# Pairs of heads, feature-major rotary queries and a shorter row of 1/rms in a two-layer attention trunk

## The chip, the cores and the metric

One core of one Trainium2 chip runs the whole program. The metric is the time of one execution on the device in microseconds, as the median of several runs. The kernel before takes 1045.22 us (median of 3 runs, 1045.22 to 1045.81).

## The reference

The input is 256 tokens of width 2048, in float32. Two layers follow each other; each has a mixer, a gate, a residual and a small per-layer embedding.

```
h = rms_norm(x); y = (mixer(h) * silu(gate(h))) @ w_out
x = x + rms_norm(y); x = x + (p @ w_pp) * sigmoid(x @ w_pg)
```

Mixer A (16 heads of 128) is stick-breaking attention without a softmax: with z the scaled scores, a key s before a query t has the weight exp(z - softplus(z) - the sum of softplus(z) over the keys between them). Mixer B (16 heads) is latent attention: queries and keys are made from normalised latents of rank 512, and each score is the sum of a 128-wide product and a 64-wide rotary product, whose key is shared by all heads:

```
q_rope = [t1 * cos - t2 * sin, t1 * sin + t2 * cos]
s = (q_nope . k_nope + q_rope . k_rope) * scale; softmax over the keys of the query's chunk and before
```

## The kernel before, in words

All matrix products that matter run in split precision: a float32 operand becomes a high part (float32r, rounded by ScalarE) and a low part (VectorE subtracts), and a product is high x high, high x low and low x high. The weights come from HBM in units of 128 x 1024 (`unit()`, lines 89 to 106): SP issues the load into one of four `raw` buffers, ScalarE makes `whi` (line 82), VectorE `wlo` (line 83); of each there are four.

Two forms of product use them. `rows()` (line 113) keeps tokens on the partitions: three matmuls (`mm3`, lines 109 to 111) with activations as the stationary operand. `cols()` (line 123) has features on the partitions: the weights are stationary and the activations move, high and low parts side by side, so that a pair of matmuls of 512 columns (line 133) and 256 columns (line 135) does the same. `halves()` (lines 146 to 151) then adds the two halves of the bank: a copy by ScalarE and a sum by VectorE.

TensorE's results go into eight banks of PSUM: four `acc` for the large products and four `att` for attention and transposes.

Layer 0: gate groups, then four groups of four heads (`group_a`, lines 355 to 368), each with 24 units of weights. Layer 1: the latents, gate groups, then four groups of four heads (`group_b`, lines 571 to 602): two units of `w_uk`, two of `w_uq`, one of `w_uqr` (the rotary queries) and two of `w_uv`. The heads of a group are worked while the next group's large products run: `weave()` (line 156) takes the products as a stream that yields after each unit, and the heads as jobs of three stages, and calls job i's stage s when `at[i] + s * LAG` units are through. The last group's heads run under the first units of the output product (`residual`, line 405).

A head of mixer A (`stick_breaking`, lines 329 to 353): scores in plain float32 (lines 333 and 334; a plain float32 matmul runs as two passes), two masks in bf16 (lines 335 and 336); ScalarE and VectorE make softplus(z), split as `sph` and `spl`; the triangle of -1 (`trir`) times both adds the sums over later keys of a block, and `nones` (all -1, plain float32) times `sp` those of the next block (line 349); exp gives the weights, `weighted_v` (line 321) the output, and `finish_head` (line 316) multiplies by the gate and splits.

A head of mixer B (`mla`, lines 539 to 569): scores in plain float32 (lines 543 and 544), masks (545 and 546), the rope product as four matmuls in float32r (548 and 549), softmax by row, transposes of the probabilities (line 565), weighted values.

The rotary queries of a group (lines 578 to 599): `rows()` leaves them with tokens on the partitions, `rotate()` (line 487) turns them in four VectorE instructions for each half of the tokens, the result is split into `qhl`, and eight transposes (line 597) bring it into feature-major form, from where ScalarE casts it into `qr`:

```
for j in range(2):
    for t in range(NT):
        nc.tensor.transpose(b[:, j * T + t * P:j * T + (t + 1) * P],
                            qhl[t][:, 2 * i + j].rearrange("p i r -> p (i r)").bitcast(F32), ident)
nc.scalar.copy(qr[:, 2 * i:2 * i + 2, :], pair(b))
```

`rstd_row()` (lines 217 to 227) lays 1/rms of the tokens along the free axis, on all partitions: ones times a diagonal, twice, so that the row stands there for two heads. It is called twice.

What orders the work: the kernel is written for a framework that keeps dependencies, buffers and semaphores. Its planner gives each engine a fixed order of instructions (`schedule_with_timeline_sim=True`, line 699): the written order is the priority, but an instruction whose operands the planner expects late by its own timing is put behind others of that engine that it expects ready. On the chip each engine then works through its order and waits where an operand is not there. The DMAs are almost all issued by SP, in such an order too.

## Time and profile before

| | us |
|---|---|
| median of the runs | 1045.22 |
| the profiled execution, its time | 1045.87 |
| its span in the profile | 1044.1 |
| busy: TensorE, VectorE, ScalarE | 1035.8, 630.6, 567.4 |

The span is the time from the first to the last instruction on the core; the execution's time has 1.8 us more around it. In the rows, PE is TensorE (its matmuls), PEld its weight loads, DVE VectorE, ACT ScalarE, POOL GpSimd and SP SyncE, which issues the transfers; a q behind the name is the engine's sequencer. L597 is line 597 of the kernel. Matmuls overlap, so a matmul's duration is longer than the distance to the next one.

### The profile page before, as it was taken

How to read it: one execution, taken by the hardware profiler on the slowest of the kernel's cores; microseconds unless marked ns; L12 is line 12 of the kernel's file. 1: busy time of each engine (PE TensorE's matmuls, PEld its weight loads, DVE VectorE, ACT ScalarE, POOL GpSimd, SP SyncE). 2: the span in 40 equal slices, each digit the busy share in tenths (PEclk: the TensorE clock that was granted, in tenths of full speed). 3: DMA queues.
4: the chain of work that ended last, by engine and by line, in shares of the span. 5: the costliest groups of instructions: out<-in, count | busy, mean ns of one | idle time of the engine just before them, and what ended most of it. 6: DMA issues, size and time to landing. Idle time of an engine off the chain costs nothing.

```text
span 1044.1 us, 14568 instructions
## 1 busy us (share of the span) xinstructions
PE 1035.8 (99%) x5563; PEld 890.4 (85%) x5563; DVE 630.6 (60%) x912; ACT 567.4 (54%) x888; POOL 6.9 (1%) x10
## 2 busy tenths in 40 slices
PE   8999999999999999999999999999999999999998
PEld 6888888888888888888888898888888888888888
DVE  7465564555655655556665576666777765558553
ACT  7654444554555556545655555665666654446442
POOL 0000000000000000000000000000000000000000
PEclk9999999999999999999999999999999999999999
DMA  8856465555555554564655485555544344655662
GB/s 305 307 169 198 166 218 185 165 173 166 163 174 168 171 191 142 180 205 150 222 181 185 129 243 185 178 191 182 183 141 136 108 150 151 205 188 183 217 209 77
DMA packets 55813, 189.03 MB, mean 181 GB/s; under 512 B 6208, under 2 KB 6976, under 8 KB 55744
## 3 DMA queue, kind: packets, MB, share of 16 engines
q1 hardware_dynamic: 55600, 188.09, 55.5%
q8 instruction: 43, 0.70, 0.3%
q14 instruction: 26, 0.21, 0.1%
q10 hardware_dynamic: 144, 0.02, 0.0%
HBM read 185.99 MB, written 2.10 MB: 180 GB/s over the span
## 4 chain that ended last, share of the span: by engine, by line
PE 96%; DMA 2%; DVE 1%; ACT 0%; issue 0%; SPq 0%; DVEq 0%
PE acc L133 24%; PE acc L109 17%; PE acc L111 17%; PE acc L110 17%; PE acc L135 12%; PE att L325 1%; DMA raw<-in_w_in_a_dram 1%; PE att L191 1%; DMA x<-in_x_dram 1%; PE att L544 1%; PE att L333 1%; PE att L326 1%; PE att L549 1%; PE att L565 0%; PE att L109 0%; PE att L111 0%
## 5 line engine op out<-in xcount | busy, mean ns | idle before, releaser
L83 DVE TENSOR_TENSOR wlo<-raw,whi 128x1024 fp32r<-128x1024 f32 (+1 forms) x295 | 355.9, 1217 | 279.9 <-ACT whi L82 272.1
L82 ACT ACTIVATE whi<-raw 128x1024 fp32r<-128x1024 f32 (+1 forms) x295 | 308.1, 1053 | 272.8 <-PE acc L111 173.3
L133 PE MATMUL acc<-actT,whi 128*128 128x512 f32 x1024 | 356.1, 398 | 1.7 <-ACT whi L82 1.1
L111 PE MATMUL acc<-whi,actT 128*128 128x512 f32 (+2 forms) x736 | 277.6, 379 | 0.0
L109 PE MATMUL acc<-whi,actT 128*128 128x512 f32 (+2 forms) x736 | 277.1, 378 | 0.0
L110 PE MATMUL acc<-wlo,actT 128*128 128x512 f32 (+2 forms) x736 | 277.0, 377 | 0.0
L135 PE MATMUL acc<-actT,wlo 128*128 128x256 f32 x1024 | 273.2, 281 | 0.1
L133 PEld LDWEIGHTS acc<-actT,whi 128*128 128x128 f32 x1024 | 189.2, 188 | 40.9 <-ACT whi L82 2.6
L135 PEld LDWEIGHTS acc<-actT,wlo 128*128 128x128 f32 x1024 | 192.6, 189 | 6.1 <-DVE wlo L83 0.7
L110 PEld LDWEIGHTS acc<-wlo,actT 128*128 128x128 f32 x736 | 138.5, 188 | 24.3
L109 PEld LDWEIGHTS acc<-whi,actT 128*128 128x128 f32 x736 | 138.4, 188 | 24.0
L111 PEld LDWEIGHTS acc<-whi,actT 128*128 128x128 f32 x736 | 138.2, 188 | 23.9
L87 DVE SCALAR_TENSOR_TENSOR wlo<-raw,pre,whi 128x512 fp32r<-128x512 f32 x80 | 55.6, 749 | 31.4 <-ACT whi L86 31.4
L86 ACT ACTIVATE whi<-raw,pre 128x512 fp32r<-128x512 f32 x80 | 52.0, 713 | 32.5 <-PE acc L133 20.0
L150 ACT COPY half<-acc 128x256 f32<-128x256 f32 x96 | 34.6, 367 | 35.3 <-PE acc L135 33.4
L133 PE MATMUL acc<-latT,whi 128*128 128x512 f32 x128 | 46.2, 401 | 0.0
L135 PE MATMUL acc<-latT,wlo 128*128 128x256 f32 x128 | 36.0, 282 | 0.0
L133 PEld LDWEIGHTS acc<-latT,whi 128*128 128x128 f32 x128 | 24.0, 188 | 5.7 <-DVE arena L151 0.4
L135 PEld LDWEIGHTS acc<-latT,wlo 128*128 128x128 f32 x128 | 24.2, 189 | 0.1
L82 ACT ACTIVATE actT<-y 128x256 fp32r<-128x256 f32 x32 | 13.3, 418 | 19.6 <-DVE y L318 19.3
L109 PE MATMUL acc<-whi,latT 128*128 128x256 f32 (+1 forms) x64 | 21.8, 340 | 0.0
L557 ACT ACTIVATE pr<-att,st 128x128 f32<-128x128 f32 (+1 forms) x32 | 13.3, 424 | 15.6 <-DVE st L555 15.6
(230 smaller groups left out, 849.2 us busy)
## 6 DMA issues: line engine op xcount, KB each, us to landing
raw<-in_w_in_a_dram SPq DMA_DIRECT2D x127, 512.0 KB, 4.2
raw<-in_w_in_b_dram SPq DMA_DIRECT2D x40, 512.0 KB, 4.4
raw<-in_w_out_a_dram SPq DMA_DIRECT2D x32, 512.0 KB, 3.6
raw<-in_w_pg_a_dram SPq DMA_DIRECT2D x32, 512.0 KB, 3.5
raw<-in_w_out_b_dram SPq DMA_DIRECT2D x32, 512.0 KB, 3.5
raw<-in_w_pg_b_dram SPq DMA_DIRECT2D x24, 512.0 KB, 4.1
raw<-in_w_dkv_dram SPq DMA_DIRECT2D x16, 288.0 KB, 3.0
raw<-in_w_pp_dram SPq DMA_DIRECT2D x8, 512.0 KB, 3.5
```

Source lines behind the costliest of these rows:

```text
L82: nc.scalar.activation(hi, src, AF.Copy)
L83: nc.vector.tensor_tensor(lo, src, hi.bitcast(F32), ALU.subtract)
L86: nc.scalar.activation(hi, src, AF.Copy, scale=gain)
L87: nc.vector.scalar_tensor_tensor(lo, src, gain, hi.bitcast(F32), ALU.mult, ALU.subtract)
L109: nc.tensor.matmul(out, lhsT=sh, rhs=mh, start=start, stop=False, **kw)
L110: nc.tensor.matmul(out, lhsT=sh, rhs=ml, start=False, stop=False, **kw)
L111: nc.tensor.matmul(out, lhsT=sl, rhs=mh, start=False, stop=stop, **kw)
L133: nc.tensor.matmul(o, lhsT=hi[:, c], rhs=aT[2][:, k].rearrange("p i t -> p (i t)"), start=k == 0, stop=False, skip_group_check=True)
L135: nc.tensor.matmul(o[:, :T], lhsT=lo[:, c], rhs=aT[0][:, k, :], start=False, stop=k == ktot - 1, skip_group_check=True)
L150: nc.scalar.copy(b, o[:, T:])
L191: nc.tensor.transpose(b[:, kk * T + t * P:kk * T + (t + 1) * P], x[:, t, k * P:(k + 1) * P], ident)
L557: nc.scalar.activation(pr[:, c], s[:, c], AF.Exp, scale=SCALE_B, bias=st[:, 1, t:t + 1], accum_out=st[:, 2, t:t + 1])
```

## The change

1. Heads go in pairs. A job is two heads, the jobs are two for each group, and `weave()` starts job i's stage s at `(i + s) * lag + 1`, with a lag of 6 units in layer 0 and of 2 in layer 1. In a stage the two heads' matmuls of one kind stand together: scores of both, masks of both, and so on. `weighted_v` puts both heads in one bank and `finish_pair` treats them in one step.
2. `nones` becomes float32r and is multiplied with `sph` and `spl` in place of `sp`.
3. The rotary queries are made feature-major: the product with `w_uqr` runs in the form of `cols()`, with the weights' columns sorted (in the split, by `by_half`) so that the first halves of the four heads' queries fill one bank and the second halves the other; the rotation is two products with a feature-major table `ropeT`, a subtraction and an addition; sixteen DMAs of 32 partitions (32 KB each) from SBUF to SBUF bring each head's halves to their partitions in `qs`, twice; `qr` is the rounded copy, its lower half of the partitions replaced by the rest. `ropeT` is made once by four transposes.
4. `rstd_row` makes the row once; those who use it broadcast it.
5. Some buffers change in number: `t256` 3 to 2, `sp` 2 to 1, `sph` and `spl` 1 to 2.

```diff
...
-    def unit(src, n=UNIT, gains=None, parts=1):
+    def unit(src, n=UNIT, gains=None, parts=1, by_half=False):
...
-        if gains is None:
+        if by_half:
+            nc.sync.dma_start(out=raw, in_=src)
+            src = raw.rearrange("p (k h i r) -> p i k h r", h=GRP, i=2, r=ROPE // 2)
+            dh, dl = (z.rearrange("p (k i h r) -> p i k h r", h=GRP, i=2, r=ROPE // 2) for z in (hi, lo))
+            for i in range(2):
+                split(dh[:, i], dl[:, i], src[:, i])
+        elif gains is None:
...
         for i, o in enumerate(banks):
-            b = tmp.tile([P, T], F32, tag="t256", name="half", bufs=3)
+            b = tmp.tile([P, T], F32, tag="t256", name="half", bufs=2)
             nc.scalar.copy(b, o[:, T:])
             nc.vector.tensor_tensor(dst[:, i, :], o[:, :T], b, ALU.add)
 
...
-    def weave(stream, jobs, at):
+    def weave(stream, jobs, lag):
+
 
         n = 0
-        steps = sorted((at[i] + s * LAG, i) for i in range(len(jobs)) for s in range(STAGES))
+        steps = sorted(((i + s) * lag + 1, i) for i in range(len(jobs)) for s in range(STAGES))
         for when, i in steps:
             while n < when and next(stream, stream) is not stream:
                 n += 1
...
         for t in range(NT):
             dg = tmp.tile([P, P], F32, tag="diag", name="diag", bufs=1)
             nc.vector.tensor_scalar(dg, ident, r[:, t:t + 1], None, ALU.mult)
-            for i in range(2):
-                nc.tensor.matmul(b[:, i * T + t * P:i * T + (t + 1) * P], lhsT=ones, rhs=dg, start=True, stop=True)
-        o = tmp.tile([P, 2, T], F32, tag="rrow", name="rrow", bufs=2)
-        nc.vector.tensor_copy(o, pair(b))
+            nc.tensor.matmul(b[:, t * P:(t + 1) * P], lhsT=ones, rhs=dg, start=True, stop=True)
+        o = tmp.tile([P, 1, T], F32, tag="rrow", name="rrow", bufs=2)
+        nc.vector.tensor_copy(o[:, 0], b[:, :T])
         return o
...
     def gate_out(g, sg, row):
         for i in range(2):
             h = sg[:, GRP * g + 2 * i:GRP * g + 2 * i + 2, :]
-            nc.vector.tensor_tensor(h, h, row, ALU.mult)
+            nc.vector.tensor_tensor(h, h, row.to_broadcast([P, 2, T]), ALU.mult)
...
+    nones = const.tile([P, P], F32R, name="nones")
+    nc.vector.tensor_scalar(nones, ones, -1.0, None, ALU.mult)
...
+    def finish_pair(h, o, sg, yT):
+        hs = slice(h, h + 2)
+        y = tmp.tile([P, 2, T], F32, tag="t512", name="y", bufs=2)
+        nc.vector.tensor_tensor(y, pair(o), sg[:, hs, :], ALU.mult)
+        split(yT[0][:, hs, :], yT[1][:, hs, :], y)
+
+    def weighted_v(v, hh, ws):
+
+        o = att()
+        for i, w in enumerate(ws):
+            c = slice((hh + i) * HD, (hh + i + 1) * HD)
+            nc.tensor.matmul(o[:, i * T:(i + 1) * T], lhsT=v[:, 0, c], rhs=w[:, :T], start=i == 0, stop=False, skip_group_check=True)
+            nc.tensor.matmul(o[:, i * T + P:(i + 1) * T], lhsT=v[:, 1, c], rhs=w[:, T:], start=False, stop=i == 1, skip_group_check=True)
         return o
...
+        zs = [att()[:, :W3] for _ in range(2)]
+        for i, z in enumerate(zs):
+            mm(z[:, :T], lhsT=k[:, hh + i, :P], rhs=q[:, hh + i, :], start=True, stop=False, skip_group_check=True)
+            mm(z[:, T:], lhsT=k[:, hh + i, P:], rhs=q[:, hh + i, P:], start=False, stop=False, skip_group_check=True)
+        for z in zs:
+            mm(z[:, :P], lhsT=identb, rhs=masks[:, :P], start=False, stop=False, skip_group_check=True)
+            mm(z[:, T:], lhsT=identb, rhs=masks[:, :P], start=False, stop=True, skip_group_check=True)
...
+            sp = tmp.tile([P, W3], F32, tag="sp", name="sp", bufs=1)
+            nc.vector.scalar_tensor_tensor(sp, z, 0.0, e, ALU.max, ALU.add)
+            sph = tmp.tile([P, W3], F32R, tag="sph", name="sph", bufs=2)
+            spl = tmp.tile([P, W3], F32R, tag="spl", name="spl", bufs=2)
+            split(sph, spl, sp)
+            parts.append((sph, spl))
         yield
-        mm(z, lhsT=trir, rhs=sph, start=False, stop=False, skip_group_check=True)
-        mm(z, lhsT=trir, rhs=spl, start=False, stop=False, skip_group_check=True)
-        mm(z[:, P:T], lhsT=nones, rhs=sp[:, T:], start=False, stop=True, skip_group_check=True)
-        w = tmp.tile([P, W3], F32, tag="w", name="w", bufs=2)
-        nc.scalar.activation(w, z, AF.Exp)
+        ws = []
+        for z, both in zip(zs, parts):
+            for x_ in both:
+                mm(z, lhsT=trir, rhs=x_, start=False, stop=False, skip_group_check=True)
+            for x_ in both:
+                mm(z[:, P:T], lhsT=nones, rhs=x_[:, T:], start=False, stop=x_ is both[1], skip_group_check=True)
...
-        finish_head(h, weighted_v(v, hh, w), sgA, yT)
+        finish_pair(h, weighted_v(v, hh, ws), sgA, yT)
...
-        weave(group_a(g, q, k, v), jobs, (1, 7, 13, 19))
-        jobs = [stick_breaking(g * GRP + hh, hh, q, k, v) for hh in range(GRP)]
+        weave(group_a(g, q, k, v), jobs, 6)
+        jobs = [stick_breaking(g * GRP + hh, hh, q, k, v) for hh in range(0, GRP, 2)]
...
-        weave(out01(range(6)), jobs, (1, 2, 4, 6))
+        weave(out01(range(6)), jobs, 2)
...
+    ropeT = [tmp.tile([P, 1, T], F32, tag="sph", name="ropeT", bufs=2) for _ in range(2)]
+    b = att()
+    for t in range(NT):
+        rt = tmp.tile([P, 2, GRP, ROPE // 2], F32, tag="t256", name="rt", bufs=2)
+        half = rope[:, t, :, ROPE // 2:].rearrange("p i (o r) -> p i o r", o=1)
+        nc.vector.tensor_copy(rt, half.to_broadcast([P, 2, GRP, ROPE // 2]))
+        for i in range(2):
+            nc.tensor.transpose(b[:, i * T + t * P:i * T + (t + 1) * P], rt[:, i].rearrange("p h r -> p (h r)"), ident)
+    for i in range(2):
+        nc.vector.tensor_copy(ropeT[i][:, 0], b[:, i * T:(i + 1) * T])
...
-    arena = big.tile([P, 2, NB], F32, tag="actT", name="arena", bufs=2)
+    arena = big.tile([P, 2 * NB + GRP * T], F32, tag="actT", name="arena", bufs=2)
+    qs = arena[:, 2 * NB:].rearrange("p (h t) -> p h t", h=GRP)
     qrT = big.tile([P, 2, GRP, T], F32R, tag="tok", name="qrT", bufs=3)
...
+        ss = [att()[:, :W3] for _ in range(2)]
+        for i, s in enumerate(ss):
+            mm(s[:, :P], lhsT=q[:, hh + i, :P], rhs=k[:, hh + i, :P], start=True, stop=False, skip_group_check=True)
+            mm(s[:, P:], lhsT=q[:, hh + i, P:], rhs=k[:, hh + i, :], start=False, stop=False, skip_group_check=True)
+        for s in ss:
+            mm(s[:, P - CHUNK:P], lhsT=identb, rhs=masks[:, P:], start=False, stop=False, skip_group_check=True)
+            mm(s[:, W3 - CHUNK:], lhsT=identb, rhs=masks[:, P:], start=False, stop=False, skip_group_check=True)
+        for i, s in enumerate(ss):
+            qp = qr[:, hh + i, :]
+            for n in range(2):
+                mm(s[:, :P], lhsT=qp[:, :P], rhs=krT[:, n, :P], start=False, stop=False, skip_group_check=True)
+                mm(s[:, P:], lhsT=qp[:, P:], rhs=krT[:, n, :], start=False, stop=n == 1, skip_group_check=True)
...
-        w = unit(a["w_uqr"][g])
-        o = [acc()[:, :T], acc()[:, :T]]
-        rows(o, cqT, w, 0, NR, T, NR)
-        qrt = tmp.tile([P, NT, GRP, ROPE], F32, tag="t512", name="qrt", bufs=2)
-        qhl = []
-        for t in range(NT):
-            rotate(qrt[:, t], o[t].rearrange("p (h r) -> p h r", h=GRP), t, GRP)
-            qhl.append(tmp.tile([P, GRP, 2, ROPE], F32R, tag="rrow", name="qhl", bufs=2))
-            split(qhl[t][:, :, 0, :], qhl[t][:, :, 1, :], qrt[:, t])
+        w = unit(a["w_uqr"][g], by_half=True)
+        o = [acc(), acc()]
+        for i, b in enumerate(o):
+            for kk in range(NR):
+                whi, wlo = (z[:, kk * T + i * P:kk * T + (i + 1) * P] for z in w)
+                nc.tensor.matmul(b, lhsT=whi, rhs=cqT[2][:, kk].rearrange("p i t -> p (i t)"), start=kk == 0,
+                                 stop=False, skip_group_check=True)
+                nc.tensor.matmul(b[:, :T], lhsT=wlo, rhs=cqT[0][:, kk, :], start=False, stop=kk == NR - 1,
+                                 skip_group_check=True)
+        qrt = tmp.tile([P, 2, T], F32, tag="t512", name="qrt", bufs=2)
+        halves(qrt, o)
+        rc = tmp.tile([P, 2, T], F32, tag="rrow", name="rc", bufs=2)
+        rs = tmp.tile([P, 2, T], F32, tag="rrow", name="rsn", bufs=2)
+        for z, i in ((rc, 0), (rs, 1)):
+            nc.vector.tensor_tensor(z, qrt, ropeT[i].to_broadcast([P, 2, T]), ALU.mult)
+        nc.vector.tensor_tensor(rc[:, 0, :], rc[:, 0, :], rs[:, 1, :], ALU.subtract)
+        nc.vector.tensor_tensor(rc[:, 1, :], rc[:, 1, :], rs[:, 0, :], ALU.add)
+        for hh in range(GRP):
+            for i in range(4):
+                r = slice(i * ROPE // 2, (i + 1) * ROPE // 2)
+                nc.sync.dma_start(out=qs[r, hh, :], in_=rc[hh * ROPE // 2:(hh + 1) * ROPE // 2, i % 2, :])
+        nc.scalar.activation(qr, qs, AF.Copy)
+        nc.vector.tensor_tensor(qr[ROPE:], qs[ROPE:], qr[ROPE:].bitcast(F32), ALU.subtract)
...
-        for i in range(GRP // 2):
-            b = att()
-            for j in range(2):
-                for t in range(NT):
-                    nc.tensor.transpose(b[:, j * T + t * P:j * T + (t + 1) * P],
-                                        qhl[t][:, 2 * i + j].rearrange("p i r -> p (i r)").bitcast(F32), ident)
...
-        weave(group_b(g, q, qr, k, v), jobs, (1, 3, 5, 6))
-        jobs = [mla(g * GRP + hh, hh, q, qr, k, v) for hh in range(GRP)]
+        weave(group_b(g, q, qr, qs, k, v), jobs, 2)
+        jobs = [mla(g * GRP + hh, hh, q, qr, k, v) for hh in range(0, GRP, 2)]
...
```

## Rows read from the trace of the kernel before

**Rows 1.** The page, part 1: busy us (share of the span), instructions.

```profile
PE 1035.8 (99%) x5563; PEld 890.4 (85%) x5563; DVE 630.6 (60%) x912; ACT 567.4 (54%) x888; POOL 6.9 (1%) x10
```

**Rows 2.** The chain of waits that ended last: share of the span by engine.

```profile
PE 96%; DMA 2%; DVE 1%; ACT 0%; issue 0%; SPq 0%; DVEq 0%
```

**Rows 3.** Busy time by stretch: us (instructions) of each engine, granted clock, DMA.

```profile
750.00:800.00 50.00, 49.52 (x317) 43.86 (x316) 36.41 (x90) 32.94 (x73) 0.00 (x0) 1.00 0.42 138
```

**Rows 4.** Timeline, TensorE: start us, us covered, instruction, count.

```profile
777.38 1.03 PE L597 MATMUL att<-c,qhl 128*128 128x128 f32 x8
```

**Rows 5.** Groups of instructions, TensorE: count | busy us, mean ns of one.

```profile
L597 PE MATMUL att<-c,qhl 128*128 128x128 f32 x32 | 4.3, 272 | 0.0
...
L224 PE MATMUL att<-diag,ones 128*128 128x128 f32 x16 | 2.6, 274 | 0.0
```

**Rows 6.** Timeline, TensorE, large products in the form of cols().

```profile
773.14 0.39 PE L133 MATMUL acc<-latT,whi 128*128 128x512 f32 x1
773.37 0.28 PE L135 MATMUL acc<-latT,wlo 128*128 128x256 f32 x1
773.48 0.40 PE L133 MATMUL acc<-latT,whi 128*128 128x512 f32 x1
```

**Rows 7.** Timeline, TensorE: masks and rope product of a head, then w_uqr.

```profile
764.38 0.19 PE L545 MATMUL att<-masks,identb 128*128 128x64 bf16 x1
764.41 0.19 PE L546 MATMUL att<-masks,identb 128*128 128x64 bf16 x1
...
764.98 0.28 PE L109 MATMUL acc<-whi,latT 128*128 128x256 f32 x1
765.10 0.28 PE L110 MATMUL acc<-wlo,latT 128*128 128x256 f32 x1
```

**Rows 8.** Timeline, TensorE: the product with nones, two matmuls before the second large one.

```profile
422.42 0.38 PE L349 MATMUL att<-sp,nones 128*128 128x128 f32 x2
...
422.87 0.40 PE L111 MATMUL acc<-whi,actT 128*128 128x512 f32 x1
```

**Rows 9.** Timeline, TensorE: a head's first mask, later its rope product.

```profile
753.52 0.19 PE L545 MATMUL att<-masks,identb 128*128 128x64 bf16 x1
...
755.98 0.22 PE L548 MATMUL att<-krT,qrT 128*128 128x128 f32 x1
...
756.44 0.28 PE L135 MATMUL acc<-latT,wlo 128*128 128x256 f32 x1
```

**Rows 10.** Timeline, TensorE: masks of a head of mixer A, then large products.

```profile
412.99 0.22 PE L335 MATMUL att<-masks,identb 128*128 128x128 bf16 x1
413.04 0.22 PE L336 MATMUL att<-masks,identb 128*128 128x128 bf16 x1
...
413.39 0.40 PE L111 MATMUL acc<-whi,actT 128*128 128x512 f32 x1
```

**Rows 11.** Groups of instructions, VectorE and ScalarE: count | busy us, mean ns.

```profile
L83 DVE TENSOR_TENSOR wlo<-raw,whi 128x1024 fp32r<-128x1024 f32 x29 | 35.5, 1224 | 16.7 <-ACT whi L82 16.6
L151 DVE TENSOR_TENSOR arena<-acc,half 128x256 f32<-128x256 f32 x27 | 10.5, 419 | 0.6 <-ACT half L150 0.5
...
L362 DVE TENSOR_TENSOR qkvA<-qkvA,rrow0q 128x512 f32<-128x512 f32 x8 | 5.5, 692 | 0.3
...
L82 ACT ACTIVATE whi<-raw 128x1024 fp32r<-128x1024 f32 x28 | 29.8, 1065 | 12.9 <-PE acc L111 6.6 <-PE acc L133 4.3 <-issue 1.3
L150 ACT COPY half<-acc 128x256 f32<-128x256 f32 x26 | 9.3, 367 | 5.1 <-PE acc L135 3.5 <-DVE actT L83 1.6
```

**Rows 12.** SP's first transfers in the timeline; groups of transfers: KB, us to landing.

```profile
2.12 0.43 SPq L262 DMA_DIRECT2D xs<-in_xT_dram  x1
2.59 0.43 SPq L98 DMA_DIRECT2D raw<-in_w_in_a_dram  x1
...
out_dram<-x SPq DMA_DIRECT2D x2, 128.0 KB, 1.9
...
raw<-in_w_uqr_dram SPq DMA_DIRECT2D x4, 512.0 KB, 4.0
```

More of the change, by code (lines that the diff above doesn't have):

```diff
@@ L42 @@
 STAGES = 3
-LAG = 2
 @with_exitstack
@@ L314, in hybrid_trunk @@
     after(exp_ln, silus[-1], "the table set of the attention comes after the gates'")
-    def finish_head(h, o, sg, yT):
-        y = tmp.tile([P, T], F32, tag="t256", name="y", bufs=3)
-        nc.vector.tensor_tensor(y, o, sg[:, h, :], ALU.mult)
-        split(yT[0][:, h, :], yT[1][:, h, :], y)
-    def weighted_v(v, hh, w):
-        o = att()[:, :T]
-        c = slice(hh * HD, (hh + 1) * HD)
-        nc.tensor.matmul(o, lhsT=v[:, 0, c], rhs=w[:, :T], start=True, stop=False)
-        nc.tensor.matmul(o[:, P:], lhsT=v[:, 1, c], rhs=w[:, T:], start=False, stop=True)
+    def finish_pair(h, o, sg, yT):
[3 more added lines that the diff above has]
+        split(yT[0][:, hs, :], yT[1][:, hs, :], y)
@@ L338, in stick_breaking @@
-        nc.scalar.activation(e, z, AF.Abs)
-        after(nc.scalar.activation(e, e, AF.Exp, scale=-1.0), exp_ln, "loaded once for all heads")
-        nc.scalar.activation(e, e, AF.Ln, bias=1.0)
-        sp = tmp.tile([P, W3], F32, tag="sp", name="sp", bufs=2)
-        nc.vector.scalar_tensor_tensor(sp, z, 0.0, e, ALU.max, ALU.add)
-        sph = tmp.tile([P, W3], F32R, tag="sph", name="sph", bufs=1)
-        spl = tmp.tile([P, W3], F32R, tag="spl", name="spl", bufs=1)
-        split(sph, spl, sp)
@@ new lines, in stick_breaking @@
+        for z in zs:
+            mm(z[:, :P], lhsT=identb, rhs=masks[:, :P], start=False, stop=False, skip_group_check=True)
+            mm(z[:, T:], lhsT=identb, rhs=masks[:, :P], start=False, stop=True, skip_group_check=True)
+        parts = []
+        for z in zs:
+            e = tmp.tile([P, W3], F32, tag="e", name="e", bufs=2)
+            nc.scalar.activation(e, z, AF.Abs)
+            after(nc.scalar.activation(e, e, AF.Exp, scale=-1.0), exp_ln, "loaded once for all heads")
+            nc.scalar.activation(e, e, AF.Ln, bias=1.0)
+            sp = tmp.tile([P, W3], F32, tag="sp", name="sp", bufs=1)
[4 more added lines that the diff above has]
+            parts.append((sph, spl))
@@ L361, in group_a @@
                 d = dst[:, 2 * i:2 * i + 2, :]
-                nc.vector.tensor_tensor(d, d, row, ALU.mult)
+                nc.vector.tensor_tensor(d, d, row.to_broadcast([P, 2, T]), ALU.mult)
         o = [acc(), acc()]
@@ L568, in mla @@
+        yield
+        ws = []
+        for pr in prs:
+            b = att()
+            for i in range(3):
+                c = slice(i * P, (i + 1) * P)
+                nc.tensor.transpose(b[:, c], pr[:, c], ident)
+            w = tmp.tile([P, W3], F32, tag="w", name="pT_", bufs=2)
+            nc.scalar.copy(w, b[:, :W3])
+            ws.append(w)
         yield
-        finish_head(h, weighted_v(v, hh, w), sgB, yT)
-    def group_b(g, q, qr, k, v):
+        finish_pair(h, weighted_v(v, hh, ws), sgB, yT)
```

60 lines of the change are left out of this document (21 added, 39 removed).

## The prediction, made before the changed kernel ran

> **What bounds the kernel now.** I read the table of engines first: TensorE is busy 99% of the span [rows 1]. Busy alone proves little, since records of matmuls overlap, so I read the chain of waits next: 96% of the path that ended last is TensorE, DMA 2%, VectorE 1% [rows 2]. Then the stretch that the change touches most: from 750 to 800 us, where mixer B's heads are worked, TensorE stands still 0.48 us of 50, while VectorE is busy 36.4 us and ScalarE 32.9 us; the granted clock is 1.00, the 2.4 GHz level [rows 3]. So the kernel is a queue of TensorE instructions with almost no holes. The change is worth what it takes out of that queue, less any hole that it opens.
>
> A duration is not a price here. Eight transposes in a row cover 1.03 us [rows 4] while one has a mean of 272 ns [rows 5]: they overlap, and one more costs (1.03 - 0.27) / 7 = 0.109 us. I therefore price by distances from start to start; a 512-column matmul holds the engine 0.23 us, with the 256-column one behind it 0.34 [rows 6]. After a block of small matmuls the first large one starts early and holds longer, so I take the start of the one behind it, less 0.23, as the block's end.
>
> **The change part by part, on TensorE.**
>
> Transposes of the rotary queries: line 597 runs 32 times [rows 5] and goes. 32 x 0.109 = **-3.5 us**. The Trainium skill's page "TensorE: Matmul & The Clock Gate" (Part 4: PE-mode transpose) gives about 275 ns for a transpose in one kernel's context. As a duration the trace agrees, with 272 ns; taken as the price, 32 would be an estimated 8.8 us and the kernel would come to 1035 us. The start-to-start distance decides against that.
>
> New transposes of the rotary table: 4, once, by the same row, **+0.4 us**. Nothing in the gate groups behind them needs them.
>
> The row of 1/rms: line 224 has 16 passes (two calls, four products each, two passes a product) [rows 5], and half go: 8 x 0.109 = **-0.9 us**.
>
> Product with w_uqr: before, per group, 24 matmuls of 256 columns at 0.12 us [rows 7], 2.88 us; after, 8 pairs of 512 and 256 columns at 0.345 us [rows 6], 2.76 us. Four groups: some **-0.5 us**.
>
> The product with nones: before, two passes of one float32 matmul, from 422.42 to 422.87 - 0.23, 0.22 us a head [rows 8]. After, two single-pass matmuls of 128 columns, on sph and spl. The nearest rows are the rope matmuls, single-pass too, of 128, 256, 128 and 256 columns: the four take 0.46 us, from 755.98 to 756.44 [rows 9], 0.115 each, though the 128-column ones have half the columns. So a short one is held at about 0.11 us, as if its weights took that long to come: 2 x 0.11 = 0.22, **0**. Bounds: at half of 0.12 the 16 heads gain 16 x 0.10 = 1.6 us; at 0.12 each they lose 0.3. I take the held value, because each stands next to another short one, as the rope matmuls do.
>
> Masks in fours in place of twos: in mixer A two masks cost 413.39 - 0.23 - 412.99 = 0.17 us, while the second starts 0.05 after the first [rows 10]. If only the step to the next kind of matmul is dear, four cost 0.28 and not 0.34: 8 pairs x 0.06 = 0.5 us at most. In mixer B two masks and the four rope matmuls take 0.60 us [rows 7]; less 0.46, two masks are 0.14, and the second starts 0.03 after the first: 8 x 0.08 = 0.6 us at most. At least the gain is 0, for no mask is added. No row shows four in a row; I take half, **-0.5 us**.
>
> Scores, weighted values and transposes of the probabilities are the same instructions in another order: 0. Sum on TensorE: -3.5 + 0.4 - 0.9 - 0.5 + 0 - 0.5 = **-5.0 us**.
>
> **Beside TensorE.** By the durations of [rows 11], per group VectorE loses eight rotate steps, four of them of half size, and two splits, some 8 x 0.42 = 3.4 us, and gets two sums of 0.42, two products of 0.69, two steps of 0.42 and a subtraction of 1024 elements, 1.22: 4.3 us. ScalarE exchanges two splits of 256 elements for two copies of 256, and two casts of 512 for one of 1024: even. Finishing heads in pairs takes one operation of 512 elements (0.69) for two of 256 (0.84), twice on VectorE. VectorE has 13 us or more of 50 free where it is fullest [rows 3], so this costs nothing; uncovered it would be 0.9 us a group. One t256 buffer less matters only when two sums are late at once, and a bank is finished every 4 x 0.345 = 1.4 us.
>
> The 16 transfers per group are new work for SP, which issues in order, 0.43 us each and 0.47 from one to the next when nothing holds them [rows 12]: 7.5 us in a group of some 28 us. Behind them wait the weight loads. These are issued far ahead, through four raw and four split buffers, each a unit of 2.8 us of TensorE's work, so a load 7.5 us late costs nothing while that lead lasts. Without it, it would cost up to 7.5 us a group.
>
> **What is late next.** A group's rotary query now takes this way after its last w_uqr matmul: half copy and sum 0.37 + 0.42, two products 1.38, subtract and add 0.84 [rows 11], the 16 issues, a landing of 1.9 (128 KB) to 4.0 us (512 KB) [rows 12], a copy of 1.07 and a subtraction of 1.22 [rows 11]. No row shows a transfer as small as 32 KB; its issue lies between nothing and 0.47 us. So the way is 7.2 to 16.8 us, and up to 1.2 us more behind a weight split at each of four handovers: 22 at the longest. The copy and the subtraction stand in the queues of ScalarE and VectorE, and a late landing also holds the half copies behind them, which free TensorE's accumulators. The cover on TensorE, in the written order: two w_uv units, 24 x 0.23 = 5.5; the next group's first w_uk unit, 8 x 0.345 = 2.8; and of the heads four weighted values and two scores at 0.66 each (six passes' worth of 0.11) and six transposes, 4.6: 13 us. That can be short. But the framework's planner orders TensorE's queue by when it expects operands: before, a head's rope matmuls stand at 755.98, 2.5 us behind its masks at 753.52, with large matmuls between [rows 9]. Three more units of 2.8 us that need no rotary query can be put in, 21 us in all. For that reason I cost the wait at nothing.
>
> **The forecast.** The profiled execution took 1045.87 us (the span of 1044.1 and 1.8 around it); less 5.0 it is 1040.9. The median of the runs lies 0.65 lower: 1045.22 - 5.0 = **1040.2 us**.
>
> **The rivals.**
>
> A, late rotary queries: slower than before. Place: the first rope matmul of each group, where the planner put it. If the planner reckons the transfers shorter than they are, TensorE's queue stands there, and ScalarE's at the copy of qs. Price: the way less the cover, at the longest 22 - 13 = 9 us a group; at half of that 4 x 4.5 = 18, less 5.0: 1058 us. It decides from a wait of (5.0 + 2.1) / 4 = 1.8 us a group. For it: queues that can't step aside. Against it: the order in [rows 9], and holes of only 0.48 us in 50 [rows 3], so the planner's times fit there now. A rule of the Trainium skill stands beside it ("DMA: Bandwidth & Descriptors", Bandwidth): gather transfers into 1 MiB, for below 64 KB they are mostly overhead; these have 32 KB. With that page's fixed 2.0 us a transfer, 16 strictly one after another would be an estimated 33 us a group. The trace speaks against such a row: loads are issued 0.47 us apart, far less than their landing takes [rows 12]. Chance 0.16.
>
> B, the gain is eaten: holes of 0.7 to 1.8 us a group at the same place, or accumulators freed late because two engines work pairs in bursts. At 1.2 us in four groups: 1045 us, no change. For it: VectorE at 73% in [rows 3]. Chance 0.15.
>
> C, more goes than I count: the matmuls with nones run at half (-1.6), the masks gain in full (-0.6 more) and the hole of 0.5 us closes: -5.0 - 2.7 = -7.7, 1037.5 us. Against it: the 0.115 us of the rope matmuls. Chance 0.09.
>
> That the change doesn't do what it says could only lie in the planner pulling the pairs apart again; that loses the 0.5 us of the masks and no more.
>
> **How the numbers follow.** The forecast has 0.60; its own range is 1038.5 to 1042.5. A difference of 0.2%, 2.1 us, is about what a measurement of this kernel can tell from no change. Faster by more: the forecast and C, 0.69. Within it: B, 0.15. Slower: A, 0.16. The range goes from 1036.5, a little under C, to 1047.5, the end of B, and leaves out A.
>
> **What would show it.** Right: no transposes of qhl, 8 passes with ones, TensorE's busy time lower by about 5 us and still 99% of the span, no wait on qr over 1 us. Wrong: TensorE standing at rope matmuls until qr, ScalarE idle before the copy of qs with a DMA as releaser, or weight loads landing just before their splits in mixer B.

## The result and the profile after

The changed kernel takes 1037.51 us (median of 6 runs, 1037.18 to 1039.54), the kernel before 1045.22 beside it (6 runs, 1045.06 to 1046.11): a ratio of 0.9929, 95% interval 0.9916 to 0.9942, or **7.7 us less**. The forecast was 1040.2, 5.0 us less. The direction and the range were right; 2.7 us of gain were not in the sum.

The profiled execution of after took 1039.29 us, with a span of 1037.5. First the table of engines, the chain that ended last and the stretch from 750 to 800 us [rows 1 to 3]:

```profile
PE 1029.2 (99%) x5495; PEld 884.1 (85%) x5495; DVE 629.2 (61%) x876; ACT 559.2 (54%) x872; POOL 6.8 (1%) x10
...
PE 97%; DMA 2%; DVE 1%; ACT 0%; issue 0%; SPq 0%; DVEq 0%
...
750.00:800.00 50.00, 50.00 (x293) 43.43 (x292) 40.72 (x86) 33.82 (x75) 0.00 (x0) 1.00 0.53 171
```

TensorE is still the queue that sets the end. It has 68 fewer passes (x5563 to x5495), 6.6 us less busy time, and in this stretch no hole at all, though VectorE is busier there (36.4 to 40.7 us of 50). The groups that the forecast priced (count | busy us, mean ns):

```profile
L622 PE MATMUL acc<-latT,whi 128*128 128x512 f32 x32 | 11.5, 397 | 0.0
...
L228 PE MATMUL att<-diag,ones 128*128 128x128 f32 x8 | 1.5, 273 | 0.0
L532 PE MATMUL att<-c,rt 128*128 128x128 f32 x4 | 0.8, 272 | 0.0
```

No transpose of rotary queries is left, the row of 1/rms has 8 passes for 16 [rows 5], the table's transposes are 4, all as counted.

**A ruler for small differences.** The executions of one kernel lie some 2 us apart (in two of the kernels below 4 and 6), and the traces show where the most of it comes from: from the start, where TensorE waits for the first weights. The first pass of the row of 1/rms, the same instruction in all kernels, starts anywhere between 54.0 and 56.1 us. Behind that, a stretch that two kernels share is the same to a few hundredths. So I cut each trace at two marks, the first matmul of the values' product of mixer A (128x512, `rows()`) and the first matmul with `w_dkv` (128x288), and compare *stretch A* (mark to mark: most of layer 0, with mixer A) and *stretch B* (second mark to the end of the span: layer 1, with mixer B). The timelines of before and, in the second fence, of after:

```profile
core 0 of [0], span 1044.1 us
...
142.91 0.40 PE L109 MATMUL acc<-whi,actT 128*128 128x512 f32 x1
...
589.26 0.29 PE L109 MATMUL acc<-whi,actT 128*128 128x288 f32 x1
```

```profile
core 0 of [0], span 1037.5 us
...
56.14 0.38 PE L228 MATMUL att<-diag,ones 128*128 128x128 f32 x2
...
143.42 0.40 PE L115 MATMUL acc<-whi,actT 128*128 128x512 f32 x1
...
588.89 0.29 PE L115 MATMUL acc<-whi,actT 128*128 128x288 f32 x1
```

Stretch A went from 446.35 to 445.47 us, **-0.9**; stretch B from 454.8 to 448.6, **-6.2**. From the first pass of the row (L228 in the second fence; at 55.26 us in before) to the first mark, 87.64 us became 87.28, another **-0.4**: 7.5 in all behind the start. The first mark is still 0.5 us later in this execution of after, which was one of its longer ones: the two profiles lie 6.6 us apart, the medians 7.7.

**Two waits are gone.** The list of TensorE's waits had two for probability transposes in mixer B before (line waited for: us in total, times, longest; `pr` are the probabilities, `pT_` their transposes), and after has none in mixer B:

```profile
PE att L325 <- ACT pT__7336 L567: 0.5, 1, 0.5
PE att L325 <- ACT pT__6987 L567: 0.5, 1, 0.5
```

The timeline of before shows one of them:

```profile
783.76 0.60 PE L325 MATMUL att<-pT__6981,arena 128*128 128x256 f32 x2
784.19 0.38 PE L326 MATMUL att<-pT__6981,arena 128*128 128x128 f32 x2
785.04 0.70 PE L325 MATMUL att<-pT__6987,arena 128*128 128x256 f32 x2 [0.46 <-ACT pT__6987 L567]
785.57 0.38 PE L326 MATMUL att<-pT__6987,arena 128*128 128x128 f32 x2
...
787.23 0.50 PE L133 MATMUL acc<-latT,whi 128*128 128x512 f32 x1
787.56 0.28 PE L135 MATMUL acc<-latT,wlo 128*128 128x256 f32 x1
```

Line 326's two passes of 128 columns hold 0.22 us from start to start; here the next start comes after 785.04 - 784.19 = 0.85. The hole is 0.63 us, but the idle time shows 0.46, because the modelled end of the matmul ahead covers the rest. With the slower restart behind it (the pair that follows takes 0.53 us to its second line where 0.43 is usual) it costs more still. The whole block, from its first probability transpose at 783.43 to 787.56 - 0.23, takes 3.9 us; its parts (three transposes, two weighted values, a head's scores, its masks and ropes) come to 2.9 by the forecast's prices. So each of the two waits costs 1.0 us, 2.0 in all. My forecast had seen one of them, as 0.48 us of idle time in 50, and left them where they were.

### The profile page after: what moved, and what is told of

It reads as the page before. It is cut to its first block, busy times and chain, and to the rows that moved or that the text cites. A ratio compares the mean times of both kernels' runs of the same rounds, so it can differ in the third digit from the quotient of the medians.

```text
span 1037.5 us, 14483 instructions
## 1 busy us (share of the span) xinstructions
PE 1029.2 (99%) x5495; PEld 884.1 (85%) x5495; DVE 629.2 (61%) x876; ACT 559.2 (54%) x872; POOL 6.8 (1%) x10
## 4 chain that ended last, share of the span: by engine, by line
PE 97%; DMA 2%; DVE 1%; ACT 0%; issue 0%; SPq 0%; DVEq 0%
PE acc L139 24%; PE acc L115 17%; PE acc L117 17%; PE acc L116 17%; PE acc L141 12%; PE att L333 1%; DMA raw<-in_w_in_a_dram 1%; PE att L196 1%; DMA x<-in_x_dram 1%; PE acc L622 1%; PE att L342 1%; PE att L334 1%; PE att L574 1%; PE att L363 1%; PE att L582 1%; PE att L603 1%
## 5 line engine op out<-in xcount | busy, mean ns | idle before, releaser
L156 ACT COPY half<-acc 128x256 f32<-128x256 f32 x104 | 37.5, 368 | 38.1 <-PE acc L141 36.3
L86 DVE SCALAR_TENSOR_TENSOR wlo<-raw,c,whi 128x576 fp32r<-128x576 f32 x16 | 13.0, 818 | 11.7 <-ACT whi L85 11.7
L85 ACT ACTIVATE whi<-raw,c 128x576 fp32r<-128x576 f32 x16 | 12.4, 776 | 12.3 <-PE acc L117 5.5
L456 ACT ACTIVATE sig<-acc 128x512 f32<-128x512 f32 (+1 forms) x18 | 9.7, 550 | 16.9 <-PE acc L117 16.5
```

Source lines behind the costliest of these rows:

```text
L85: nc.scalar.activation(hi, src, AF.Copy, scale=gain)
L86: nc.vector.scalar_tensor_tensor(lo, src, gain, hi.bitcast(F32), ALU.mult, ALU.subtract)
L156: nc.scalar.copy(b, o[:, T:])
```

## Experiments

Each kernel ran beside the kernel before. "After" in the table is the changed kernel; the other kernels are named in the text below. Ratios are to before, with the 95% interval.

| kernel | median, us | ratio | A, us | B, us |
|---|---|---|---|---|
| before | 1045.22 | 1 | 446.4 | 454.8 |
| after | 1037.51 | 0.9929 (0.9916 to 0.9942) | 445.5 | 448.6 |
| u_rot | 1040.82 | 0.9959 (0.9946 to 0.9971) | 445.5 | 451.9 |
| u_row | 1039.25 | 0.9941 (0.9929 to 0.9954) | 445.5 | 449.3 |
| u_mask | 1038.80 | 0.9938 (0.9924 to 0.9951) | 445.2 | 449.2 |
| u_nones | 1037.06 | 0.9921 (0.9907 to 0.9934) | 445.1 | 448.6 |
| b_at | 1043.16 | 0.9977 (0.9966 to 0.9988) | 446.4 | 452.6 |
| d_dma | 1057.45 | 1.0115 (1.0100 to 1.0130) | 445.5 | 467.7 |
| u_pairB | 1052.77 | 1.0079 (1.0064 to 1.0093) | 445.5 | 465.8 |
| u_pairB_at | 1041.48 | 0.9960 (0.9945 to 0.9975) | 445.5 | 452.0 |
| u_pairB_early | 1047.43 | 1.0016 (1.0003 to 1.0028) | 445.5 | 459.1 |
| u_pairB_pool | 1050.61 | 1.0049 (1.0035 to 1.0063) | 445.5 | 460.6 |
| u_pairB_both | 1049.71 | 1.0046 (1.0029 to 1.0063) | 445.5 | 460.0 |
| best | 1034.64 | 0.9897 (0.9883 to 0.9910) | 443.4 | 448.1 |

### u_rot: the rotary part undone

```diff
-        w = unit(a["w_uqr"][g], by_half=True)
...
-                nc.sync.dma_start(out=qs[r, hh, :], in_=rc[hh * ROPE // 2:(hh + 1) * ROPE // 2, i % 2, :])
+        w = unit(a["w_uqr"][g])
+        o = [acc()[:, :T], acc()[:, :T]]
+        rows(o, cqT, w, 0, NR, T, NR)
...
+                    nc.tensor.transpose(b[:, j * T + t * P:j * T + (t + 1) * P],
+                                        qhl[t][:, 2 * i + j].rearrange("p i r -> p (i r)").bitcast(F32), ident)
```

> Undoes the rotary part alone: heads stay in pairs and the row is made once, but the rotary queries are token-major again, with 8 transposes a group, and no table is transposed and no small transfer made. Theory (the gain is the terms on TensorE's queue plus two waits of before for the probability transposes, about 1 us each, which the pairs closed): the transposes come back (32 x 0.109 = +3.5 us), the four of the table go (-0.4), the product costs +0.2 as the blocks of the two traces have it; the two waits stay away: 1037.5 + 3.3 = 1040.8 us, 0.9957 of before. Rival (the two waits went because the rotary part took work off ScalarE and VectorE in mixer B): they return, +2.0 more, 1042.8 us, 0.9977.

1040.82 us: the theory's number. Mark and span in its timeline:

```profile
core 0 of [0], span 1039.0 us
...
587.12 0.29 PE L115 MATMUL acc<-whi,actT 128*128 128x288 f32 x1
```

Stretch B is 451.9, 3.3 us longer than after, and no wait in mixer B is in the list. So, with the heads in pairs, the rotary part is worth what it takes off TensorE's queue and no more, and the two waits did not go with it.

### u_row: the row made twice again

```diff
-            nc.tensor.matmul(b[:, t * P:(t + 1) * P], lhsT=ones, rhs=dg, start=True, stop=True)
+            for i in range(2):
+                nc.tensor.matmul(b[:, i * T + t * P:i * T + (t + 1) * P], lhsT=ones, rhs=dg, start=True, stop=True)
```

> The row of 1/rms is made twice again: four matmuls of 128 columns more in all, 8 passes, their results unused; all else as after. Theory: 8 x 0.109 = +0.9 us, 1038.4 us, 0.9935 of before, and in the trace each block of the row doubles. Rival (the row stood in a gap of the start where TensorE waits for weights anyway): 0, 1037.5 us, 0.9926.

1039.25 us; the interval holds the theory's 0.9935 and not the rival's 0.9926. The second row lies in stretch B, which is 0.7 us longer; the first lies ahead of stretch A, from 56 us on. Its first pass and the first mark:

```profile
56.12 0.38 PE L229 MATMUL att<-diag,ones 128*128 128x128 f32 x2
...
143.65 0.40 PE L115 MATMUL acc<-whi,actT 128*128 128x512 f32 x1
```

From the first pass to the first mark it is 87.53 us here, and 87.28 in after and in the ten other kernels below that are built on it. 0.25 and 0.7 make 0.9: the price for both rows stands, though not as two equal halves.

### u_mask: masks behind each head's own scores

```diff
-        for z in zs:
             mm(z[:, :P], lhsT=identb, rhs=masks[:, :P], start=False, stop=False, skip_group_check=True)
             mm(z[:, T:], lhsT=identb, rhs=masks[:, :P], start=False, stop=True, skip_group_check=True)
...
-        for s in ss:
             mm(s[:, P - CHUNK:P], lhsT=identb, rhs=masks[:, P:], start=False, stop=False, skip_group_check=True)
             mm(s[:, W3 - CHUNK:], lhsT=identb, rhs=masks[:, P:], start=False, stop=False, skip_group_check=True)
```

> Pairs kept, but each head's two masks stand right behind its own scores again, in both mixers. Theory (masks gain in full when four stand in a row): +0.45 in mixer A and +0.6 in mixer B, 1038.5 us, 0.9936 of before. Rival (half of it, as forecast, the rest being where the planner put other work): +0.5, 1038.0 us, 0.9931.

1038.80 us, too close to both numbers to choose; the stretches do. B is 0.6 us longer, the full gain of the masks of mixer B. The timeline of after shows why it is full:

```profile
792.67 0.19 PE L576 MATMUL att<-masks,identb 128*128 128x64 bf16 x1
792.70 0.19 PE L577 MATMUL att<-masks,identb 128*128 128x64 bf16 x1
...
792.76 0.19 PE L577 MATMUL att<-masks,identb 128*128 128x64 bf16 x1
792.79 0.31 PE L581 MATMUL att<-krT,qrT 128*128 128x128 f32 x1
792.93 0.34 PE L582 MATMUL att<-krT,qrT 128*128 128x256 f32 x1
793.11 0.22 PE L581 MATMUL att<-krT,qrT 128*128 128x128 f32 x1
793.17 0.33 PE L582 MATMUL att<-krT,qrT 128*128 128x256 f32 x1
```

Masks follow at 0.03 us; what is dear is the step into the next kind, the first rope matmul, held 0.14 us where the later one of 128 columns is held 0.06. A pair pays it once. In mixer A the opposite came out: a block of scores and four masks is 0.05 us longer there with masks apart, but the whole stretch A is 0.3 us *shorter*. The planner orders the work of the last group otherwise there (a pair's block of scores and masks is taken apart, from 397.6 us on), and I put the difference down to that.

### u_nones: plain float32 again

```diff
-    nones = const.tile([P, P], F32R, name="nones")
+    nones = const.tile([P, P], F32, name="nones")
...
-            for x_ in both:
-                mm(z[:, P:T], lhsT=nones, rhs=x_[:, T:], start=False, stop=x_ is both[1], skip_group_check=True)
+            mm(z[:, P:T], lhsT=nones, rhs=sp[:, T:], start=False, stop=True, skip_group_check=True)
```

> After the change with one part undone: the matrix of -1 is plain float32 again and one matmul of two passes takes the unsplit softplus, in place of two single-pass matmuls on its halves (the softplus stays in the tile of its exponential, for room). Theory (a short single-pass matmul is held by its weight load at about 0.11 us, so the two cost what the two passes did): 0, 1037.5 us, 0.9926 of before, and the block of triangle and these matmuls at 573 ns a head in the trace, as after. Rival (the half of the third case of the prediction): +1.6 us, 1039.1 us, 0.9942.

1037.06 us, nothing lost. In the timeline of after the two single-pass matmuls:

```profile
412.05 0.22 PE L365 MATMUL att<-sph,nones 128*128 128x128 f32 x1
412.11 0.28 PE L365 MATMUL att<-spl,nones 128*128 128x128 f32 x1
412.22 0.45 PE L117 MATMUL acc<-whi,actT 128*128 128x512 f32 x1
```

The second holds 0.11 us, and the next kind starts behind it as late as behind two passes: a whole block of two heads' triangles, these products and the next pair's scores and masks takes 2.74 us in both kernels. Stretch A is even 0.4 us shorter with plain float32. As the blocks are equal, I put that down to placement, which no run here shows.

### b_at: the kernel before, heads written two at a time

```diff
-        weave(group_b(g, q, qr, k, v), jobs, (1, 3, 5, 6))
+        weave(group_b(g, q, qr, k, v), jobs, (1, 1, 3, 3))
...
-        weave(out01(range(6)), jobs, (1, 2, 4, 6))
+        weave(out01(range(6)), jobs, (1, 1, 3, 3) if i else (1, 2, 4, 6))
```

> The kernel before with one thing changed: in mixer B the steps of its single heads are written two at a time (1, 1, 3, 3 instead of 1, 3, 5, 6). Theory (the two waits for probability transposes came from where the written order puts the heads' steps): they go, -2.0 us: 1043.2 us, 0.998 of before. Rival (they come from single heads as such, and only pairs close them): 1045.2 us, both waits still in the list.

1043.16 us, the theory's number. All of TensorE's waits, then mark and span:

```profile
PE att L251 <- DVE zeros L169: 1.2, 1, 1.2
PE acc L133 <- ACT whi L82: 0.6, 1, 0.6
```

```profile
core 0 of [0], span 1041.3 us
...
588.67 0.29 PE L109 MATMUL acc<-whi,actT 128*128 128x288 f32 x1
```

The numbers of two lists close both waits, with single heads and the old rotary part, and shorten stretch B from 454.8 to 452.6, by 2.2 us. So this part of the gain belongs to the order in which the heads are written and needs nothing that pairs share. (With the new rotary part that is not all that pairs do: see u_pairB_at.)

### d_dma: the small transfers doubled

```diff
-                nc.sync.dma_start(out=qs[r, hh, :], in_=rc[hh * ROPE // 2:(hh + 1) * ROPE // 2, i % 2, :])
+                for t in range(NT):
+                    ts = slice(t * P, (t + 1) * P)
+                    nc.sync.dma_start(out=qs[r, hh, ts], in_=rc[hh * ROPE // 2:(hh + 1) * ROPE // 2, i % 2, ts])
```

> After the change with the small transfers doubled: each of the 16 a group is issued as two halves of 128 columns, 32 a group, so that SyncE issues for some 20 us a group instead of 10, and the rotary queries come some 10 us later. Theory (the pairs' order leaves more cover than the chain needs): 0 to +1 us, 1037.5 to 1038.5 us, 0.9926 to 0.9936 of before. Rival (the cover is all but used up at 19 us of chain): +5 us or more, 1042 us and above, with a window of lower clock in mixer B as in the run with single heads.

1057.45 us: the theory falls and the rival holds, at four times its least price. Waits of TensorE and ScalarE, SP's issues in the first group, and a stretch:

```profile
PE att L581 <- DVE qrT L641: 10.8, 4, 6.7
...
ACT qrT L640 <- DMA arena<-rc: 14.3, 4, 6.2
```

```profile
746.93 21.15 SPq L639 DMA_DIRECT2D arena<-rc  x32
768.18 0.53 SPq L104 DMA_DIRECT2D raw<-in_w_uv_dram  x1
```

```profile
760.00:780.00 20.00, 13.30 (x60) 11.05 (x59) 10.42 (x21) 8.79 (x16) 0.00 (x0) 0.83 0.38 125
```

32 issues take SP 21 us, weight loads stand behind them, and TensorE stands at the first rope matmul of a group until the query is there, 10.8 us in all. It is the forecast's rival A, with the marks that it named: TensorE at the rope matmuls, ScalarE before the copy with a DMA as releaser. Of the 20 us from 760 TensorE is busy 13.3, and behind that hole the granted clock of the stretch is 0.83: part of it ran at 1.2 GHz. All of TensorE's waits in mixer B make 13 of the 19 us by which stretch B is longer than after's; the other 6, the time at the lower clock among them, are not taken apart.

How near was the changed kernel itself? Its timeline, for the first group (SyncE, ScalarE, VectorE, then TensorE's first rope matmul):

```profile
748.67 10.11 SPq L637 DMA_DIRECT2D arena<-rc  x16
...
760.74 1.06 ACT L638 ACTIVATE qrT<-arena 128x1024 fp32r<-128x1024 f32 x1
...
761.84 1.22 DVE L639 TENSOR_TENSOR qrT<-arena,qrT 64x1024 fp32r<-64x1024 f32 x1 [0.56 <-ACT qrT L638]
...
765.89 0.22 PE L581 MATMUL att<-krT,qrT 128*128 128x128 f32 x1
```

The query is there at 763.06 and used at 765.89: 2.8 us to spare. In the other groups it is 4.4, 6.2 and 8.3. The way from the start of the last `w_uqr` matmul took 19.1 to 24.0 us, and the planner had set the rope matmuls 22 to 28 us behind it.

### u_pairB and its four variants: single heads in mixer B

u_pairB has the stages of before in mixer B:

```diff
-        weave(group_b(g, q, qr, qs, k, v), jobs, 2)
-        jobs = [mla(g * GRP + hh, hh, q, qr, k, v) for hh in range(0, GRP, 2)]
+        weave_at(group_b(g, q, qr, qs, k, v), jobs, (1, 3, 5, 6))
+        jobs = [mla(g * GRP + hh, hh, q, qr, k, v) for hh in range(GRP)]
```

> Undoes the pairs in mixer B alone: one head per job there, in the order of before, with everything else as after the change. Theory: the masks of mixer B lose what four in a row give (+0.6 us) and the two waits for the probability transposes come back (+2.0): 1040.1 us, 0.9951 of before. Rival (the waits went with the rotary part): only +0.6, 1038.1 us, 0.9932.

1052.77 us, beyond both: the rotary part and single heads in the old order don't go together. (Its trace is of an execution of 1055.33 us, near the longest, so its stretch B stands high.) Two views, a stretch and SP's issues:

```profile
780.00:800.00 20.00, 18.31 (x75) 14.48 (x74) 10.48 (x31) 9.61 (x27) 0.00 (x0) 0.61 0.30 109
```

```profile
769.69 10.23 SPq L652 DMA_DIRECT2D arena<-rc  x16
780.02 0.52 SPq L104 DMA_DIRECT2D raw<-in_w_uv_dram  x1
```

From 774 to 795 us TensorE's order holds steps of heads and not one large matmul; they wait for each other through ScalarE and VectorE, and the clock falls to 0.61. A "busy" of 18.3 us hides that: at the lower clock the same matmul counts longer (a mask 0.26 us at 780.34, where the rows of after above have 0.19). Four runs asked what makes the heads crowd. In the first, u_pairB_at, the order changes, here against u_pairB:

```diff
-        weave_at(group_b(g, q, qr, qs, k, v), jobs, (1, 3, 5, 6))
+        weave_at(group_b(g, q, qr, qs, k, v), jobs, (1, 1, 3, 3))
...
-        (weave_at(out01(range(6)), jobs, (1, 2, 4, 6)) if i else weave(out01(range(6)), jobs, 2))
+        (weave_at(out01(range(6)), jobs, (1, 1, 3, 3)) if i else weave(out01(range(6)), jobs, 2))
```

> The kernel with mixer B's heads single, which came to 1052.8 us, with the heads' steps written two at a time (units 1, 1, 3, 3 of the stream instead of 1, 3, 5, 6), as the pairs have them. Theory now (in 1, 3, 5, 6 the steps of the later heads fall behind the group's last units, where a rotary chain that ends later lets four heads crowd with nothing large between them; in 1, 1, 3, 3 they don't): the crowding goes, what stays is the masks' 0.6 us: 1038.1 us, 0.9932 of before, and no window with a granted clock under 1. Rival (the single heads' chains themselves are the trouble, whatever their order): 1050 us or more, and a window at half clock again.

1041.48 us, 3.4 above the theory's number and far below the rival's: 11.3 of the 15.3 us are back by the order alone, and the clock is 1.00 throughout mixer B. Stretch B stays 3.4 us longer than after: 0.6 for the masks, and 2.0 of idle time in these waits, all between 780 and 787 us, at the probability transposes (L619), the weighted values (L358) and the rope matmuls (L602):

```profile
PE att L619 <- DVE pr L614: 1.1, 2, 0.7
...
PE att L358 <- ACT pT__6924 L621: 0.6, 1, 0.6
...
PE att L602 <- DVE qrT L654: 0.3, 1, 0.3
```

So beside the new rotary part, in the same order, pairs are worth 2.8 us more than their masks. The theory had left that out.

In u_pairB_early, in the old order, the whole block of the rotary queries moves to the head of `group_b`, ahead of the loop over `w_uk` and `w_uq`:

> The same kernel with single heads in the old order 1, 3, 5, 6, but the rotary queries' product, their transfers and copies stand first in the group's stream, ahead of the keys' and queries' units, so that they are there some 11 us (four units of 2.8 us) earlier. If the late rotary queries are what crowds the heads (the first rival of the prediction): the crowding goes, 1040 us, 0.995 of before (masks 0.6 and the two waits of before 2.0 remain). Rival (the order alone does it, or the chain's load on ScalarE and VectorE): above 1048 us again.

1047.43 us (1044.54 to 1050.30): in between. The second group's queries are there 18.6 us ahead of their first rope matmul now, and from 780 to 790 us TensorE is busy 6.5 of 10 all the same. In u_pairB_pool only the queue changes:

```diff
-                nc.sync.dma_start(out=qs[r, hh, :], in_=rc[hh * ROPE // 2:(hh + 1) * ROPE // 2, i % 2, :])
+                nc.gpsimd.dma_start(out=qs[r, hh, :], in_=rc[hh * ROPE // 2:(hh + 1) * ROPE // 2, i % 2, :])
```

> The kernel with mixer B's heads single in the old order (1052.8 us), its 64 small transfers issued on GpSimd's queue, which has nothing else to do in mixer B, instead of SyncE's. There the trace has SyncE issuing 16 transfers from 769.7 to 779.9 us and four loads of weights behind them, from 780.0 on, while TensorE has only heads left and its granted clock falls to 0.61. If the queue is the cause (weights late, so that large matmuls are missing between the heads): 1040 us, 0.995 of before (masks 0.6, the two waits 2.0), no window of lower clock. If late rotary queries or the heads' own chains are: above 1047 us again.

1050.61 us. Landing takes 3.9 us there, for 1.9 on SP's queue, so the queries come later still (25.7 us behind the last `w_uqr` matmul in the second group, for 21.5), while the weights no longer stand behind the transfers. The granted clock is 1.00 all through mixer B, and stretch B is 12.0 us longer than after's all the same: most of such a loss needs no lower clock. u_pairB_both has both edits:

> The last two edits on single heads in the old order together: the rotary queries' product and transfers stand first in the group's stream, and the transfers are issued on GpSimd's queue. Each alone left the time well above 1040 us (1047.4 with the product first, 1050.6 with the other queue). If the lateness of the queries and the 10 us for which SyncE's queue is taken are together what the rotary part costs the single heads: 1040 to 1041 us, 0.995 to 0.996 of before, and no window with TensorE below 19 of 20 us. If the old order of single heads crowds whatever the queries do: above 1045 us again.

1049.71 us, and in stretch B 11.4 us more than after. By the medians earlier queries give back 5 of the 15 us, the other queue 2 and both together 3: neither explains the crowding, while the order gave back 11. Why the planner crowds single heads in the order 1, 3, 5, 6 with the new rotary part and doesn't with the old one stays open.

### best: a version that beats both

```diff
-        zs = [att()[:, :W3] for _ in range(2)]
+        z0 = pair(att())
+        z1 = pair(att()[:, :T])
...
+        m = masks[:, :P].rearrange("p (o t) -> p o t", o=1).to_broadcast([P, 2, P])
+        mm(z0[:, :, :P], lhsT=identb, rhs=m, start=False, stop=False, skip_group_check=True)
+        mm(z1, lhsT=identb, rhs=m, start=False, stop=True, skip_group_check=True)
...
+        for x_ in (sph, spl):
+            mm(z0[:, :, P:], lhsT=nones, rhs=x_[1], start=False, stop=x_ is spl, skip_group_check=True)
...
+    rT = tmp.tile([P, 2, T], F32, tag="sph", name="ropeT", bufs=1)
+    nc.sync.dma_start(out=rT, in_=pair(a["ropeT"]))
```

> After the change with two things more. Mixer A's pair shares its banks by key block (one bank of 2x256 columns for the first key block of both heads, one of 2x128 for the second), so that masks and the products with -1 are two matmuls of 256 columns in place of four of 128. The table of the rotation comes feature-major from the host's table of cosines and sines in one load, in place of four transposes. Theory: products with -1 from 0.46 to 0.24 us a pair, 8 pairs, -1.8; masks -0.3; transposes -0.4: 1035.0 us, 0.9902 of before. Rival (256 columns are as slow as two of 128, or the pair's one long chain of ScalarE and VectorE in mixer A comes late): -0.4 or worse, 1037.1 us and above.

1034.64 us, 2.9 below after and 10.9 below before. Its timeline, in a pair of mixer A:

```profile
187.55 0.28 PE L366 MATMUL att<-sph,nones 128*128 128x256 f32 x1
187.67 0.28 PE L366 MATMUL att<-spl,nones 128*128 128x256 f32 x1
187.78 0.59 PE L343 MATMUL att<-qkvA 128*128 128x256 f32 x2
```

Both heads' products with -1 take 0.23 us, where after needs as much for each head (0.17 to the next start, and the slower start behind it). Stretch A is 2.1 us shorter and B 0.5, as the theory had it (1.8 + 0.3, and 0.4).

## Why the prediction was right, and where its sum was not

- **The rotary part, right.** -3.5, +0.4 and -0.5 make 3.6; the trace with that part undone says 3.3. The price of 0.109 us a transpose from start to start held. The `w_uqr` product gave 0.2 by its block (11.48 to 11.25 us over the four groups), not 0.5.
- **The row, right:** 0.9, by 0.25 and 0.7.
- **nones, right at 0.** The value from the nearest row, a short single-pass matmul held at 0.11 us, was met (412.11 to 412.22), and undoing it costs nothing. What holds it there no run shows.
- **Masks, half in the sum, full on the chip** in mixer B (0.6 for about 0.3), by the mechanism in the upper bound. In mixer A the blocks gained, but the stretch is 0.3 shorter with the masks apart.
- **The step that failed: "scores, weighted values and transposes of the probabilities are the same instructions in another order: 0".** The order closed two holes of mixer B. I knew one of them, as 0.48 us of idle time in 50 [rows 3], and put its closing into rival C, at 0.5. Changing the order alone gave 2.2. Idle time is counted from modelled ends, so a hole has to be measured from start to start, against what those instructions hold elsewhere.
- **Rival C had the right total by partly wrong terms:** the masks and the holes came, the half-priced products with nones did not. Rotary part 3.3, order 2.2, masks of mixer B 0.6 and the second row 0.7 make 6.8 beside the measured 6.2 of stretch B. They need not add up: the order was measured on the kernel before and the others by undoing them in after, and beside the new rotary part the order is worth 11.3. That C's number is the measured one is therefore partly luck. The 0.9 us of stretch A aren't settled: the blocks of masks say 0.4, and two experiments moved that stretch by 0.3 and 0.4, which I put down to placement.
- **Rival A did not come, but was nearer than 0.16 may sound.** The bound on an issue, nothing to 0.47 us, was wrong: it took 0.63 from one to the next. With that and what stood ahead of it on its engines, the way was 19 to 24 us and not 7.2 to 16.8, in one group longer than the 22 that I called the longest. The cover was longer too, 22 to 28 us where I had allowed 21. That the planner would make room was the right reason; that 2.8 us were left in the first group was luck as far as my numbers go. With the transfers doubled the price was 19 us. (The 15 us of u_pairB are another matter: earlier queries brought back 5 of them.) The Trainium skill fits a fixed cost of 2.0 us to a transfer that GpSimd issues ("DMA: Bandwidth & Descriptors", Anatomy of one DMA); as a landing the traces have 1.9 us on SP's queue, and 3.9 on GpSimd's (u_pairB_pool). As a price of each of 16 in a row, an estimated 33 us a group, it isn't borne out: they took 10.1 us of issues, and the landings ran under the issues that followed.

## What to carry to other kernels

Before costing a reorder at nothing, look for each wait of the bottleneck engine in the trace, measure it from start to start, and ask whether the new order closes it; here the numbers of two lists were worth 2.2 us. A chain of small transfers that is hidden today should be tested by doubling it: 3 us of slack and 19 us of loss lay one doubling apart. And where a matmul of 128 columns is held as long as one of 256, 0.11 to 0.12 us as in float32r here, put two heads side by side in one bank and use 256 columns.

## What the runs showed of the hardware

- A transfer of 32 KB from 32 partitions to 32 others within SBUF takes SP longer to issue than a load of 512 KB from HBM: 0.59 us in the median, with 507 to 1052 ns, against 0.33. With 128 columns rather than 256 it gets no cheaper: 32 take 21.15 us, 0.66 each. In the view of the line that issues them, and a load in the timeline:

```profile
L637 SPq DMA_DIRECT2D arena<-rc x64: 507/589/1052, 748.7 to 836.4; - x64
...
DMA to landing us min/median/max: 1.8/1.9/3.4
```

```profile
742.93 0.33 SPq L95 DMA_DIRECT2D raw<-in_w_uqr_dram  x1
```

- Nine kernels that share stretch A agree on its length to 0.03 us (445.47 to 445.49), while whole executions differ by 2 us. Stretch B of after and of u_nones, whose layer 1 is the same, differs by 0.02. So differences of 0.2 us can be read from single traces behind the start; that this holds where heads crowd is not shown, and the 10 executions of u_pairB_early lie up to 5.8 us apart.
